# A three-mixer network with expert layers: the overflow branch moved into the block, small loads moved into the mixers, a token tile split earlier

## The chip, the cores and the metric

The kernel runs on one core of a Trainium2 chip. The metric is the time of one execution on the device in microseconds (us), median of several runs. A profile is one further execution, recorded by the hardware profiler.

## The reference, cut to what matters

256 tokens with 1024 features go through three layers. Each layer is a mixer (attention and recurrences of several kinds) followed by a mixture of experts, and the result is normalised once more. The mixers are called even, odd and second here, after the kernel's methods.

```python
for layer in range(2):                       # first_block: even mixer, then odd mixer
    h = _rms(x, norm1_w[layer]) * (1 + scale1) + shift1
    x = x + gate1 * mixer(h)                 # projections, attention, output projection
    h = _rms(x, norm2_w[layer]) * (1 + scale2) + shift2
    x = x + gate2 * _hier_moe(h, ...)        # 32 experts
x = x + second_mixer(rmsnorm(x, attn_norm))  # second_block
x = x + hier_moe(rmsnorm(x, ffn_norm), ...)  # 32 experts again
return rmsnorm(x, final_norm)
```

The experts: a token picks one of 4 groups and in it the best 2 of 8 experts. Each expert e computes `(silu(h @ w1[e]) * (h @ w3[e])) @ w2[e]` with matrices of 1024 x 512, 1024 x 512 and 512 x 1024 floats, 6 MB an expert and 201 MB a layer, all of which is read.

## The kernel before, in words

**Ring and loads.** Weights and large activations share a ring of 18 slots of 1 MB (`ring`, tiles named `slot`). `plan` puts loads on a list in the order of their use, through all layers; `pump` writes the next ones into the program as long as `free > reserve`, all issued by SP (SyncE, L193). `release(n, reserve)` gives n slots back and reserves some of them for activations that will ask for a slot later, `done` gives back the slots of used weights. A load waits on the chip until the last reader of its slot is through.

**Order of landings.** The framework lets eight DMAs be under way. Each DMA, of SP's queue and of ScalarE's, takes the next of eight semaphores in turn, in the order of the program, and waits until the DMA that had it before has landed. Small loads (router weights, constants, the bias) are issued by ScalarE with `nc.scalar.dma_start` and take their turns in the same order.

**A mixer** (`even`, `odd`, `second`) is written by `weave`, which takes steps of several generators (one `stream` of projections, others for heads and normalisations) by estimated costs. `prep` splits weights into a high and a low part (ScalarE, VectorE and GpSimd, L460 to L462) ahead of TensorE's use, up to three chunks ahead. Its last part is `out_last`, the second half of the output projection, token tile 0 and then token tile 1 (tiles of 128 tokens); with token tile 1, `route_turn` and `route_logits` transpose tile 0 and compute its router logits. The transposed tokens hT take one slot.

**An expert block** (`moe`) begins with the reciprocal root of the mean square of all 256 tokens, transposes and router logits of tile 1, and the tokens scaled and split into a high part `hh` and a low part `hl`, one slot each: both high halves on ScalarE (L1775), the low half of tile 0 on GpSimd in two steps (L1778, L1779), that of tile 1 on VectorE (L1782, called `rest`, ahead of the ranks). `route` finds groups, experts and each token's rank within its expert on VectorE, with `warm` multiplications on TensorE between; `finish` computes the weights of the pairs and the largest rank `ti`.

Each expert has room for 64 tokens (`CAP`). `onehot` makes selection matrices for 4 experts, and `gather` multiplies the tokens' halves with them: 32 multiplications on 256 columns give the tokens of 2 pairs of experts, `xg`. If a rank reaches 64, `overflow` computes the remaining tokens of all experts in a loop. It stands between `gather(0)` and the first pair, in a branch on a value which every engine reads:

```python
rv = nc.values_load(ti, min_val=0, max_val=T, ...)
with tc.If(rv >= CAP):
```

The branch isn't taken with these inputs. Behind it every engine adds to semaphores what the body would have added; for the semaphores of DMAs SP does so, each after waiting for its last landing. The body of before has more DMAs than there are semaphores, so all eight are waited for.

Then come 16 pairs of experts. Pair p: `up(p, "g")` (L1840 is its silu), the first half of `combine(p - 1)`, `up(p, "u")` (its end is VectorE's L1844), with odd p `gather` for the next two pairs, `gather_w`, `turn`, the other half of `combine(p - 1)`, `down(p)`. An "up" or "down" has 32 multiplications of 64 columns of weights by 512, and gives its four slots back two at a time, half way and at the end. `parts` splits the result of "down" (VectorE, ScalarE and GpSimd, L1863 to L1865), `combine` multiplies it back to token order and VectorE adds it to x (L1891). At pair 0, behind the first `up`, `start()` is called:

```python
def start1():
    n.gate_coeffs(1, 5)
    n.router(2)
    n.second_setup(pre)
```

`gate_coeffs` broadcasts a row with TensorE and ScalarE, `router` issues 4 small loads, `second_setup` 11 (L1131). `start0` has the bias of the odd mixer (`bias_load`, 1 MB), `gate_coeffs` and `router(1)`. In the third block one load of the final norm's weights stands there.

## Time and profile before

| | |
|---|---|
| median of 3 runs | 2110.97 us (2109.19 to 2112.38) |
| the profiled execution | 2108.36 us |
| its span, first to last instruction | 2106.3 us |
| mean granted TensorE clock, share of full speed | 0.968 |
| TensorE busy | 1901.6 us (90%) |
| VectorE, ScalarE, GpSimd busy | 858.1, 427.5, 327.9 us |
| moved by DMA | 725.35 MB, mean 344 GB/s |

PE is TensorE, PEld its loading of weights, DVE VectorE, ACT ScalarE, POOL GpSimd, SP SyncE; a q behind an engine means its sequencer, which waits, branches and issues DMAs while the engine itself may be busy or idle. Times count from the start of the span. A matrix product in full precision appears as two MATMUL rows.

### The profile page before, as it was taken

To read this page: it belongs to the slowest core of one execution; us is meant where nothing else is said; L and a number is where in the kernel's file an instruction comes from. 1 tells how busy PE (TensorE), PEld (TensorE's weight loads), DVE (VectorE), ACT (ScalarE), POOL (GpSimd) and SP (SyncE) were. 2 spreads that over 40 slices of the span, in tenths; PEclk is the share of its full clock that TensorE was granted. 3 is DMA by queue.
4 is the path that set the end of the run, shared out by engine and by line. 5 is a ranking of instruction groups with operands and counts; after the bars stand their busy time and mean duration, and the time that the engine had idled before them with its cause. 6 is when DMAs were issued, how large, how long until landed. Compare 5 with 4: busy or idle time off the path is not lost. (4 is left out here: it accounts for less than half of the span.)

```text
span 2106.3 us, 24926 instructions
## 1 busy us (share of the span) xinstructions
PE 1901.6 (90%) x9930; PEld 1056.1 (50%) x9930; DVE 858.1 (41%) x1574; ACT 427.5 (20%) x778; POOL 327.9 (16%) x248
## 2 busy tenths in 40 slices
PE   6888799999999899899999999998899899999997
PEld 3656344444444667534444444586788344444443
DVE  3665333333322567533332232467666333232223
ACT  1423101111100343211110011254544111010011
POOL 1331100000000334100000000142444000000000
PEclk8998899999999999999999999998999999999999
DMA  9697799999999856799999999921357799999997
GB/s 323 238 319 297 260 422 421 422 421 421 421 421 406 300 222 244 294 365 421 421 421 421 421 421 421 326 101 41 125 194 300 292 421 421 421 421 422 421 421 285
DMA packets 157547, 725.35 MB, mean 344 GB/s; under 512 B 25305, under 2 KB 43088, under 8 KB 85226
## 3 DMA queue, kind: packets, MB, share of 16 engines
q1 hardware_dynamic: 139216, 716.84, 84.9%
q10 hardware_dynamic: 18201, 6.76, 1.3%
q8 instruction: 85, 1.39, 0.3%
q14 instruction: 45, 0.36, 0.0%
HBM read 722.48 MB, written 1.07 MB: 344 GB/s over the span
## 5 line engine op out<-in xcount | busy, mean ns | idle before, releaser
L257 PE MATMUL ps<-slot,xg 128*64 128x512 f32 x2992 | 710.5, 599 | 20.6 <-DMA slot<-moe_w 9.6
L257 PEld LDWEIGHTS ps<-slot,xg 128*64 128x64 f32 x2992 | 254.4, 138 | 422.0 <-issue 359.8
L257 PE MATMUL ps<-slot,ht 128*64 128x512 f32 (+1 forms) x1552 | 345.0, 574 | 56.4 <-issue 49.2
L257 PE MATMUL ps<-slot 128*128 128x256 f32 (+8 forms) x2230 | 368.4, 327 | 15.1 <-DVE slot L461 9.6
L257 PEld LDWEIGHTS ps<-slot 128*128 128x128 f32 (+3 forms) x2230 | 300.5, 187 | 73.6 <-issue 14.0
L257 PEld LDWEIGHTS ps<-slot,ht 128*64 128x64 f32 x1552 | 128.7, 139 | 228.4 <-issue 213.9
L1891 DVE TENSOR_TENSOR x<-x,ps 128x512 f32<-128x512 f32 x180 | 115.3, 682 | 277.0 <-PE ps L257 277.0
L1865 POOL TENSOR_TENSOR yl<-sg,yh 128x512 fp32r<-128x512 f32 (+1 forms) x68 | 82.5, 1213 | 884.8 <-ACT yh L1864 884.8
L462 POOL TENSOR_TENSOR slot<-slot 128x512 fp32r<-128x512 f32 (+2 forms) x108 | 164.4, 1539 | 273.2 <-ACT slot L460 261.9
L1844 DVE SCALAR_TENSOR_TENSOR hh<-sg,ws,ps 128x512 f32<-128x512 f32 x48 | 53.4, 1113 | 319.4 <-PE ps L257 179.8
L1864 ACT CAST yh<-sg 128x512 fp32r<-128x512 f32 (+1 forms) x68 | 40.3, 593 | 468.9 <-DVE sg L1863 468.9
L461 DVE TENSOR_TENSOR slot<-slot 128x512 fp32r<-128x512 f32 (+2 forms) x108 | 110.2, 1035 | 54.4 <-ACT slot L460 53.9
L1863 DVE TENSOR_TENSOR sg<-ps,ga 128x512 f32<-128x512 f32 (+1 forms) x68 | 44.9, 660 | 175.2 <-PE ps L257 175.2
L460 ACT CAST slot<-slot 128x1024 fp32r<-128x1024 f32 (+2 forms) x108 | 106.6, 1020 | 46.2 <-PE ps L257 27.3
L257 PEld LDWEIGHTS ps<-u,slot 128*128 128x128 f32 x768 | 96.9, 199 | 18.3 <-issue 17.0
L257 PE MATMUL ps<-u,slot 128*128 128x256 f32 x768 | 101.9, 293 | 0.0
L1840 ACT ACTIVATE sg<-ps 128x512 f32<-128x512 f32 x48 | 28.7, 598 | 312.4 <-PE ps L257 312.4
L257 PE MATMUL ps<-yh,pg 128*128 128x512 f32 (+1 forms) x204 | 87.1, 429 | 0.7 <-ACT yh L1864 0.7
L257 PE MATMUL ps<-yl,pg 128*128 128x512 f32 (+1 forms) x204 | 77.5, 382 | 0.9 <-POOL yl L1865 0.8
L1916 POOL TENSOR_TENSOR slot<-x,rows 128x512 f32<-128x512 f32 x2 | 2.5, 1272 | 464.5 <-DVE x L1912 464.5
L398 ACT ACTIVATE xg<-ps,cf 128x256 f32<-128x256 f32 x64 | 36.2, 565 | 156.6 <-PE ps L257 156.6
L1867 ACT CAST yh<-ps 128x512 fp32r<-128x512 f32 (+1 forms) x34 | 19.1, 561 | 227.3 <-PE ps L257 227.2
(334 smaller groups left out, 1586.4 us busy)
## 6 DMA issues: line engine op xcount, KB each, us to landing
slot<-moe_w SPq DMA_DIRECT2D x376, 1024.0 KB, 19.8
slot<-w_gate SPq DMA_DIRECT2D x59, 1024.0 KB, 17.7
slot<-w_up SPq DMA_DIRECT2D x59, 1024.0 KB, 19.8
slot<-w_down SPq DMA_DIRECT2D x50, 1024.0 KB, 18.1
slot<-ada_w SPq DMA_DIRECT2D x48, 1024.0 KB, 7.7
slot<-w_in SPq DMA_DIRECT2D x20, 1024.0 KB, 8.5
slot<-odd_w_in SPq DMA_DIRECT2D x12, 1024.0 KB, 13.1
more<-w_down SPq DMA_DIRECT2D x10, 1024.0 KB, 19.8
```

Source lines behind the costliest of these rows:

```text
L257: self.nc.tensor.matmul(out, lhsT=lhsT, rhs=rhs, start=start, stop=stop)
L398: self.nc.scalar.activation(out, p, AF.Identity, scale=a, bias=nb[:, k:k + 1])
L460: nc.scalar.copy(wh, src)
L461: nc.vector.tensor_sub(wl[:, 0], src[:, 0], wh[:, 0].bitcast(FT))
L462: nc.gpsimd.tensor_sub(wl[:, 1], src[:, 1], wh[:, 1].bitcast(FT))
L1840: nc.scalar.activation(sg, ps, AF.Silu)
L1844: nc.vector.scalar_tensor_tensor(ha.rearrange("s k p -> s p k"), st["sg", p].rearrange("s (p k) -> s p k", k=4), st["ws", p], ps.rearrange ...
L1863: nc.vector.tensor_mul(y, ps, self.ga[:, sl])
L1864: nc.scalar.copy(yh, y)
L1865: nc.gpsimd.tensor_sub(yl, y, yh.bitcast(FT))
L1867: nc.scalar.copy(yh, ps)
L1891: nc.vector.tensor_add(self.x[:, t, sl], self.x[:, t, sl], ps)
```

## The change

The diff does these things.

- **Branch.** `overflow` moves from the front of a block to behind pair 5 (`LATE`). There both halves of `combine(5)` and the gather for pairs 6 and 7 come around it. Its body is rewritten: the transposed tokens go into an `xg` tile, and three loads in a loop replace the earlier ones. hT's slot is given back right behind the router logits.
- **Split.** The slots of `hh` and `hl` are taken in `out_last`. Tile 0's root, high part (ScalarE) and low part (VectorE, two halves) are computed while tile 1 is projected. Tile 1's high part follows on ScalarE, its low part on VectorE in two halves, one before the ranks and one behind the first `onehot`. GpSimd has no part in it.
- **Gather.** `gather(0)` is split into pair 0's columns (before `finish`) and pair 1's (behind `up(0, "u")`). `warm(1)` behind the ranks becomes `warm(2)`.
- **Small loads.** `bias_load` goes into the even mixer, `router(1)` and `second_setup` into the odd one, `router(2)` and the final norm into the second.
- **Reserve.** Three slots are reserved ahead of `out_last` where it was one, and none at the end of a mixer where it was two.

```diff
@@ -26,6 +26,7 @@
 NEG = -1e30
 E = 32
 CAP = 64
+LATE = 5
 RING = 18
 SLOT = 2048
 SCRATCH = 2048
@@ -521,6 +522,8 @@
         setup = self.route_setup()
         next(setup)
         self.hT = self.slot().rearrange("p (k q) -> p k q", k=KC)
+        self.hs = [self.slot(FR).rearrange("p (t k q) -> p t k q", t=NT, k=KC) for i in range(2)]
+        self.hr = self.cp.tile([P, NT], FT, name="xr", bufs=2)
         for t in range(NT):
             for n in range(2):
                 p = self.psum()
@@ -537,9 +540,29 @@
                 self.out_sink(t, n, gate, True)(p)
                 if not t and not n:
                     next(setup)
+                if n and not t:
+                    self.token_rstd(0)
+                    self.token_high(0)
                 if t:
                     (self.route_logits if n else self.route_turn)(0)
+                    self.token_low(0, 4 * n)
                     yield (1.8, 0.0)
+        self.token_rstd(1)
+
+    def token_rstd(self, t):
+        r = self.hr[:, t:t + 1]
+        self.nc.vector.tensor_reduce(r, self.ssq[:, t, :2], axis=AX.X, op=OP.add)
+        self.rstd(r, r, D)
+
+    def token_high(self, t):
+        xv = self.x[:, t].rearrange("q (p k) -> q k p", k=KC)
+        self.nc.scalar.activation(self.hs[0][:, t], xv, AF.Copy, scale=self.hr[:, t:t + 1])
+
+    def token_low(self, t, k):
+        xv = self.x[:, t].rearrange("q (p k) -> q k p", k=KC)
+        hh, hl = self.hs
+        self.nc.vector.scalar_tensor_tensor(hl[:, t, k:k + 4], xv[:, k:k + 4], self.hr[:, t:t + 1],
+                                            hh[:, t, k:k + 4].bitcast(FT), op0=OP.mult, op1=OP.subtract)
 
     def plan_cols(self, key, w, c0, n):
         src = w.rearrange("(p k) n -> p k n", k=KC)[:, :, c0:c0 + n]
@@ -782,7 +805,7 @@
                        p.rearrange("p (h q) -> p h q", h=4))
             yield (0.9, 0.0)
         self.flag("ob", 1.5)
-        self.release(4, reserve=1)
+        self.release(4, reserve=3)
 
     def swa(self, g, bias, sc):
         nc, A = self.nc, self.A
@@ -939,6 +962,7 @@
                 self.gate_coeffs(0, 2)
                 yield (1.8, 5.0)
                 self.router(0)
+                self.bias_load(1, self.bias1)
                 yield from self.mix(self.slab_tm(512, s_vb), 8, self.ev[2])
                 yield from self.mix(self.slab_tm(512, s_rb), 8, self.ev[3])
                 self.release(2)
@@ -958,7 +982,7 @@
             self.weave(self.gla(g, q), self.bias_tile(0, bias, sc), self.swa(g, bias, sc),
                        self.swa_tile(g, 1), self.swa_tile(g, 0),
                        stream())
-        self.release(5, reserve=2)
+        self.release(5)
 
 
     def plan_odd(self):
@@ -1062,6 +1086,8 @@
                 self.outputs(8)
                 yield from self.mix(self.slab_tm(512, s_v(4)), 8, self.od[1])
                 self.gate_coeffs(1, 2)
+                self.router(1)
+                self.second_setup(self.pre)
                 yield (3.8, 0.3)
                 yield from self.mix(self.slab_tm(512, s_qk(3)), 8, self.od[2])
                 yield from self.mix(self.slab_tm(512, s_qk(1)), 8, self.od[3])
@@ -1074,12 +1100,12 @@
                 yield from self.out_half([(self.o[0][:, h], self.o[1][:, h]) for h in range(4)], True)
                 self.prep()
                 yield tuple(("o", h) for h in range(4, 8))
-                self.release(3, reserve=1)
+                self.release(3, reserve=3)
                 yield from self.out_last([(self.o[0][:, h], self.o[1][:, h]) for h in range(4, 8)], True)
 
             self.qkt = {}
             self.weave(*[transposed(s) for s in (2, 0, 3, 1)], *[head(h) for h in range(8)], stream())
-        self.release(6, reserve=2)
+        self.release(6)
 
 
     def plan_second(self):
@@ -1542,6 +1568,7 @@
                 yield from t(h, KC, [[(f, 0, P, s_kraw(1)), (0, P, 152, s_vv(1, 0)), (1, P, 152, s_vv(1, 1))]])
                 self.outputs(4)
                 self.outputs(4)
+                self.router(2)
                 yield from self.slab_fm(4, s_q)
                 yield from self.slab_fm(4, s_f)
                 yield from self.slab_fm(4, s_hq)
@@ -1559,15 +1586,16 @@
                 yield ("hg",)
                 self.mx = [self.slot(FR).rearrange("p (c t) -> p c t", c=8) for i in range(2)]
                 yield from branch(self.o[2:], 1)
-                self.release(3, reserve=1)
+                self.release(3, reserve=3)
                 coeffs()
+                nc.scalar.dma_start(self.rows[1], self.A["final_norm_2"].rearrange("(o n) -> o n", o=1).to_broadcast([P, D]))
                 yield (5.0, 0.0)
                 m = [(self.mx[0][:, k], self.mx[1][:, k]) for k in range(8)]
                 yield from self.out_half(m[:4], False)
                 yield from self.out_last(m[4:], False)
 
             self.weave(self.nsa_prep(g), self.nsa_attn(g, sc), self.hgrn(g, q8), stream())
-        self.release(6, reserve=2)
+        self.release(6)
 
 
     def plan_moe(self, l):
@@ -1669,7 +1697,7 @@
         self.mm(p[:, 0], self.ltri, mk[:, 0], True, True)
         self.mm(p[:, 1], self.ones, mk[:, 0], True, False)
         self.mm(p[:, 1], self.ltri, mk[:, 1], False, True)
-        self.warm(1)
+        self.warm(2)
         rk = g.tile([P, NT, E], FT, name="rk")
         nc.vector.scalar_tensor_tensor(rk, p, 1.0, mk, op0=OP.add, op1=OP.mult)
         nc.vector.tensor_scalar(rk, rk, -1.0, None, op0=OP.add)
@@ -1710,17 +1738,16 @@
         for i in range(n):
             self.mm(p[:, :476], self.ident, self.km, True, True)
 
-    def overflow(self, g, l, hT, h, rk, wt, ti, w1, w3, w2, gate):
+    def overflow(self, g, l, h, rk, wt, ti, w1, w3, w2, gate):
         nc, tc = self.nc, self.tc
-        wd = self.dp.tile([E, P, NT], FT, name="wd", tag="wd")
         rv = nc.values_load(ti, min_val=0, max_val=T, skip_runtime_bounds_check_because="rank < T")
         with tc.If(rv >= CAP):
             wv = g.tile([P, NT, E], FT, name="wv")
             nc.vector.tensor_scalar(wv, rk, float(CAP), None, op0=OP.is_ge)
             nc.vector.tensor_mul(wv, wv, wt)
+            cnt = g.tile([P, 1], FT, name="top")
+            hT = g.tile([P, KC, T], FT, name="xg")
...
+                with tc.For_i(0, 4, 1) as c:
+                    for p, w, tag in zip(pp, (w1, w3), ("yh", "yl")):
+                        nc.scalar.dma_start(wt_, w[bass.ds(e, 1)]...)
...
+                    nc.scalar.dma_start(wt_, w2[bass.ds(e, 1)]...)
...
     def moe(self, l, mods, start, coeffs, slots, fill=None):
         nc, tc = self.nc, self.tc
         _, w1, w3, w2, gate = self.moe_args(l)
         with tc.tile_pool(name="moe", bufs=1, reuse_waits="tile") as g:
-            hT = self.hT
-            hh, hl = (self.slot(FR).rearrange("p (t k q) -> p t k q", t=NT, k=KC) for i in range(2))
-            r = self.x_rstd()
+            hh, hl = self.hs
+            r = self.hr
             self.route_turn(1)
+            self.token_high(1)
             self.route_logits(1)
-            xv = self.x.rearrange("q t (p k) -> q t k p", k=KC)
-            for t in range(NT):
-                nc.scalar.activation(hh[:, t], xv[:, t], AF.Copy, scale=r[:, t:t + 1])
-            h0 = g.tile([P, KC, 2 * P], FT, name="xg").rearrange("p (t k) q -> p t (k q)", t=NT)[:, 0]
-            h0 = h0.rearrange("p (k q) -> p k q", k=KC)
-            nc.gpsimd.tensor_scalar(h0, xv[:, 0], r[:, 0:1], None, op0=OP.mult)
-            nc.gpsimd.tensor_sub(hl[:, 0], h0, hh[:, 0].bitcast(FT))
-
-            def rest():
-                nc.vector.scalar_tensor_tensor(hl[:, 1], xv[:, 1], r[:, 1:2], hh[:, 1].bitcast(FT),
-                                               op0=OP.mult, op1=OP.subtract)
-
-            rk, wt, ti, finish, late = self.route(g, r, mods, rest)
+            self.release()
+            rk, wt, ti, finish, late = self.route(g, r, mods, lambda: self.token_low(1, 0))
             NP = E // 2
             st = {}
             if l == 2:
@@ -1801,18 +1818,19 @@
                 nc.vector.tensor_mul(uw, u, bc(wt, 2 * p, 2))
                 st["uw", p] = uw
 
-            def gather(j):
-                xg = g.tile([P, KC, 2 * P], FT, name="xg")
+            def gather(j, c=slice(0, 2 * P)):
+                if c.start == 0:
+                    st["xg"] = g.tile([P, KC, 2 * P], FT, name="xg")
+                xg = st["xg"]
                 u = st["u", j].rearrange("p t a s -> p t (a s)")
                 for k0 in range(0, KC, 2):
-                    ps = self.psum().rearrange("p (k s) -> p k s", k=2)
+                    ps = self.psum().rearrange("p (k s) -> p k s", k=2)[:, :, :c.stop - c.start]
                     for k in range(2):
                         for t in range(NT):
                             for i, part in enumerate((hh, hl)):
-                                self.mm(ps[:, k], part[:, t, k0 + k], u[:, t], t + i == 0, t + i == 2)
+                                self.mm(ps[:, k], part[:, t, k0 + k], u[:, t, c], t + i == 0, t + i == 2)
                     for k in range(2):
-                        self.affine(xg[:, k0 + k], ps[:, k], k0 + k, "av"[k])
-                st["xg"] = xg
+                        self.affine(xg[:, k0 + k, c], ps[:, k], k0 + k, "av"[k])
 
             def gather_w(p):
                 ps = self.psum((P, T))
@@ -1922,13 +1940,11 @@
                 add(3)
 
             onehot(0)
+            self.token_low(1, 4)
+            gather(0, slice(0, P))
             finish()
-            gather(0)
             if late is not None:
                 late()
-            self.pump()
-            self.overflow(g, l, hT, (hh, hl), rk, wt, ti, w1, w3, w2, gate)
-            self.release()
             weighted(0)
             for p in range(NP):
                 last = p == NP - 1
@@ -1946,26 +1962,30 @@
                     turn(p)
                 else:
                     up(p, "g")
-                    if p:
+                    if p and p - 1 != LATE:
                         combine(p - 1, 0)
-                    else:
+                    elif not p:
                         gather_w(0)
                         start()
-                        if l == 2:
-                            nc.scalar.dma_start(fw, self.A["final_norm_2"].rearrange("(o n) -> o n", o=1)
-                                                .to_broadcast([P, D]))
                     up(p, "u")
-                    if p % 2:
+                    if not p:
+                        gather(0, slice(P, 2 * P))
+                    if p % 2 and p != LATE:
                         gather(p // 2 + 1)
                         if p == NP - 3:
                             self.release(2, reserve=min(2, slots))
                     gather_w(p + 1)
                     turn(p)
-                    if p:
+                    if p and p - 1 != LATE:
                         combine(p - 1, 1)
                 if fill is not None:
                     fill(p)
                 (down_last if last else down)(p)
+                if p == LATE:
+                    combine(p, 0)
+                    combine(p, 1)
+                    self.overflow(g, l, (hh, hl), rk, wt, ti, w1, w3, w2, gate)
+                    gather(p // 2 + 1)
                 if p == NP - 2:
                     coeffs()
             if l == 2:
@@ -2007,30 +2027,17 @@
         n.plan_moe(2)
 
         n.reserve = 6
-        n.even(lambda: n.norm_coeffs(0, 7, 3, 4))
-
         bp = ctx.enter_context(ExitStack())
         n.bias1 = bp.enter_context(tc.tile_pool(name="bias", bufs=1, side="right")).tile([P, 8, T], FT, name="bias1")
-
-        def start0():
-            n.bias_load(1, n.bias1)
-            n.gate_coeffs(0, 5)
-            n.router(1)
-
-        n.moe(0, n.ev[6], start0, lambda: n.norm_coeffs(1, 6, 0, 1), 8,
+        n.even(lambda: n.norm_coeffs(0, 7, 3, 4))
+        n.moe(0, n.ev[6], lambda: n.gate_coeffs(0, 5), lambda: n.norm_coeffs(1, 6, 0, 1), 8,
               lambda p: 4 <= p < 8 and n.bias_flip(n.bias1, n.bias1, p - 4))
+        pb = ctx.enter_context(ExitStack())
+        n.pre = pb.enter_context(tc.tile_pool(name="pre", bufs=1))
         n.odd(lambda: n.norm_coeffs(1, 7, 3, 4))
         bp.close()
         n.rb.close()
-        pb = ctx.enter_context(ExitStack())
-        pre = pb.enter_context(tc.tile_pool(name="pre", bufs=1))
-
-        def start1():
-            n.gate_coeffs(1, 5)
-            n.router(2)
-            n.second_setup(pre)
-
-        n.moe(1, n.od[5], start1, lambda: n.norm_coeffs(1, 8), 14)
+        n.moe(1, n.od[5], lambda: n.gate_coeffs(1, 5), lambda: n.norm_coeffs(1, 8), 14)
         n.fb.close()
         n.second(lambda: n.norm_coeffs(1, 9))
         pb.close()
```

## Rows read from the trace of the kernel before

**Rows 1.** Windows: us, busy us by engine, granted clock, DMA share, GB/s
```profile
224.00:256.00 32.00, 24.64 (x105) 10.16 (x105) 7.42 (x15) 4.75 (x7) 0.00 (x0) 0.86 0.66 235
260.00:670.00 410.00, 381.57 (x1802) 170.91 (x1800) 127.04 (x196) 43.90 (x74) 38.32 (x30) 1.00 1.01 421
876.00:906.00 30.00, 24.02 (x110) 8.80 (x110) 6.94 (x14) 3.87 (x6) 0.00 (x0) 1.00 0.74 251
1630.00:1650.00 20.00, 14.45 (x67) 9.15 (x67) 11.19 (x35) 4.55 (x8) 1.90 (x1) 0.83 0.28 105
```

**Rows 2.** Timeline, VectorE, L1844: start, duration us, shapes [idle before, releaser]
```profile
305.75 1.09 DVE L1844 SCALAR_TENSOR_TENSOR hh<-sg,ws,ps 128x512 f32<-128x512 f32 x1 [6.29 <-issue]
361.31 1.09 DVE L1844 SCALAR_TENSOR_TENSOR hh<-sg,ws,ps 128x512 f32<-128x512 f32 x1 [6.29 <-issue]
...
687.04 1.09 DVE L1844 SCALAR_TENSOR_TENSOR hh<-sg,ws,ps 128x512 f32<-128x512 f32 x1 [2.87 <-PE ps L257]
951.37 1.09 DVE L1844 SCALAR_TENSOR_TENSOR hh<-sg,ws,ps 128x512 f32<-128x512 f32 x1 [6.29 <-issue]
...
1333.33 1.08 DVE L1844 SCALAR_TENSOR_TENSOR hh<-sg,ws,ps 128x512 f32<-128x512 f32 x1 [2.83 <-PE ps L257]
1714.37 1.09 DVE L1844 SCALAR_TENSOR_TENSOR hh<-sg,ws,ps 128x512 f32<-128x512 f32 x1 [6.29 <-issue]
...
2083.07 1.08 DVE L1844 SCALAR_TENSOR_TENSOR hh<-sg,ws,ps 128x512 f32<-128x512 f32 x1 [3.19 <-PE ps L257]
```

**Rows 3.** Waits of SP, 880 to 912 us: releaser, us in total, times, longest
```profile
SPq L193 <- DMA br<-b_grp: 11.1, 1, 11.1
...
SPq L193 <- DMA k_vmask<-k_vmask: 6.9, 1, 6.9
```

**Rows 4.** Waits of SP, 236 to 262 us
```profile
SPq L193 <- DMA bias<-bvec: 6.8, 1, 6.8
```

**Rows 5.** Timeline of the first block's start, 186 to 262 us
```profile
213.55 2.07 DVE L1649 TENSOR_TENSOR oh<-km,i 128x16 f32<-128x16 f32 x1
...
216.68 0.17 DVE L1649 TENSOR_TENSOR oh<-km,i 128x16 f32<-128x16 f32 x1
...
217.25 2.06 DVE L1782 SCALAR_TENSOR_TENSOR slot<-x,xr,slot 128x1024 fp32r<-128x1024 f32 x1
...
218.14 1.04 PE L257 MATMUL ps<-km 128*128 128x476 f32 x2
...
221.09 6.19 PE L257 MATMUL ps<-u,slot 128*128 128x256 f32 x32
...
231.44 9.40 PE L257 MATMUL ps<-slot,xg 128*64 128x512 f32 x32 [4.15 <-issue]
```

**Rows 6.** Timeline of TensorE, 1374 to 1378 us
```profile
1375.16 1.46 PE L257 MATMUL ps<-wx,slot 128*128 128x152 f32 x12
```

**Rows 7.** Timeline of the third block's start
```profile
1645.85 7.09 PE L257 MATMUL ps<-slot,xg 128*64 128x512 f32 x32 [1.82 <-DVEq L1717]
```

**Rows 8.** Source line L1717, the branch: shortest, median, longest ns, first and last start
```profile
L1717 PEldq COMPARE_BRANCH  x3: 3578/3798/3818, 224.9 to 1641.6; - x3
```

**Rows 9.** The page's groups: busy us, mean ns, idle before
```profile
L1865 POOL TENSOR_TENSOR yl<-sg,yh 128x512 fp32r<-128x512 f32 (+1 forms) x68 | 82.5, 1213 | 884.8 <-ACT yh L1864 884.8
```

**Rows 10.** Waits of SP, 380 to 412 us
```profile
SPq L193 <- DMA slot<-moe_w: 27.2, 13, 2.1
```

**Rows 11.** Timeline of ScalarE, 98 to 106 us
```profile
103.51 2.00 ACT L460 CAST slot<-slot 128x1024 fp32r<-128x1024 f32 x2 [2.63 <-DMA wr<-moe_w_expert]
```

**Rows 12.** Timeline of ScalarE, 896 to 902 us: first and last of eleven
```profile
896.04 0.44 ACTq L1131 DMA_DIRECT2D k_rope<-k_rope  x1
...
901.48 0.34 ACTq L1131 DMA_DIRECT2D ll<-hg_lb_logits  x1
```

**Rows 13.** Timeline of the odd mixer, ScalarE and TensorE
```profile
767.26 1.24 ACT L248 COPY pT<-ps 128x384 f32<-128x384 f32 x3 [0.18 <-PE ps L267]
...
769.11 2.17 PE L257 MATMUL ps<-pT,slot 128*128 128x128 f32 x18
```

57 lines of the change are left out of this document (27 added, 30 removed).

## The prediction

> **What bounds the kernel now.** I read the page first and then DMA by stretch, the expert pairs, the queue of the loads, the route, and the mixers' ScalarE. There are three mixers, each followed by an expert block, and the expert blocks are the long plateaus. Inside one the loads move 421 GB/s without a break [rows 1], so a 1 MB load takes 1.049/421 = 2.49 us and a pair of experts (12 loads) 29.9 us. TensorE needs less. Between the pairs 2 and 4 of the first block, at a time when the ring is still full, the step that ends "up" comes 361.31 − 305.75 = 55.6 us apart, 27.8 a pair [rows 2]. From pair 2 to pair 15 that would be 13 × 27.8 = 361 us, and it takes 381.3, 382.0 and 368.7 us in the three blocks [rows 2]. So TensorE waits about 20, 21 and 8 us for weights in the later pairs: the end of a block is set by its last load, and what counts is how early the loads become continuous. Time that TensorE loses early is free up to those 20, 21 and 8 us.
>
> Before each plateau the loads limp: 235 GB/s over 32 us at the first block, 251 over 30 at the second, 105 over 20 at the third [rows 1]. At 421 this is (421−235)/421 × 32 = 14.1 us of idle DMA, 12.1 and 15.0. Two causes. All slots are full and the first is given back only half way through the first "up", and in the first two blocks SP then stands still: every load waits for the landing of the DMA eight before it, of whatever queue, and the small loads that ScalarE issues there take places in this order. SP waited 11.1 and 6.9 us for them at the second block [rows 3], 6.8 us for bias1 at the first [rows 4].
>
> **The start of a block.** In the first block, GpSimd's subtraction holds up a VectorE step to 2.07 us where the same instruction takes 0.17 later; without GpSimd −1.9. The low half of token tile 1 costs 2.06 us ahead of the ranks; half of it stays there, −1.0. Ranks are then 2.9 us earlier, but a second warm-up multiplication (1.04 us) now stands between them and the gather, so this starts some 2.6 us earlier. It took 6.19 us, 193 ns a multiplication, with the granted clock at its lower level for part of it (0.86 over the stretch, rows 1) [rows 1, 5]. The first half has the same 32 multiplications on 128 columns; the nearest row, 152 columns, has twelve in 1.46 us, 122 ns [rows 6], and with the overlap at its end I take 110, 3.5 us: −2.7. Then TensorE idled 4.15 us at the branch [rows 5]; in its place come the last affine step, the maximum of the ranks and one small multiplication, some 1.5 us: −2.65. Against this, tile 0's high part (I take the present 2.1 us on ScalarE) comes ahead of ScalarE's copies in the last projections, and a VectorE half of 1.0 us ahead of the last reduction: +1.1. The first "up" begins 6.9 us earlier, and runs in 7.09 as in the third block instead of 9.40 [rows 5, 7]. In the third block clock and branch cost less (there TensorE's pause is 1.82 us, rows 7), and the same terms give −4.2. Bounds: 0 (if the ScalarE work costs 4) to 9 us.
>
> What does it give? First block: 14.1 us idle, plus the 2.5 of bias1, which leaves this stretch, minus 5.0 for two loads that the larger reserve (3 slots, not 1) pushes into it: 11.6. The late gather half adds 3.5 us of TensorE but covers 1.5 us of waiting for VectorE; it delays the "down" slots by 2, still in time for the DMA. Second block: 12.1 + 2.2 for the 0.9 MB of small loads − 5.0 + about 1 us of idle DMA before that stretch: 10 (bounds 5 to 13). Third: no small load held SP, so the loads gain the 4.2 us and 1.2 of the final norm's half MB, 5.4, if TensorE follows.
>
> The Trainium skill (TensorE: Matmul & The Clock Gate, "Back-to-back issue gap") says that streaming time goes with the number of columns, with a sustained spacing of 81 ns at 128. By it a half gather takes 2.6 us, an estimate, and the third block gains 0.9 us more; the trace's 152-column row speaks against it, and my sum goes by the row.
>
> **The late branch.** TensorE's branch instruction takes 3.6 to 3.8 us [rows 8], now partly covered by queued multiplications. At pair 5 it stands behind "combine", which itself waits for the parts of "down": VectorE, then ScalarE, then GpSimd's 1.2 us [rows 9], some 3 us uncovered; then about 3.5 us of branch, and the gather behind it no longer covers VectorE's step (1.0). I sum 7.5 us (5.8 in the third block, where the parts are shorter); bounds 4 and 12, with 2.3 us of slower clock as in rows 5. Behind the branch wait the gather and "up" of pair 6. Cover: TensorE's waiting later in the block. First block: 20 + 6.9 − 2 − 7.5 = 17, more than the 11.6 gained, and likewise in the second, so all of it stays. Third: 8 + 4.2 − 2 − 5.8 = 4.4, less than 5.4, so 4.4. SP branches too, and waits there for three places of the order of eight, the oldest; in this stretch it waits for landings of its own loads anyway (27.2 of 32 us) [rows 10], so five stay in flight, 12 us of data, and DMA doesn't pause.
>
> **The small loads in the mixers.** In the odd mixer ScalarE issues 4 router loads (2.6 us of waiting ScalarE in the even mixer, which issues its own already) [rows 11] and 11 for the last mixer (896.04 to 901.82, 5.8 us) [rows 12] right behind the gate copies. That is 8.4 us in which ScalarE starts nothing. Queued behind: a weight cast of 1.05 us and the copies pT, at 767.26 now, and TensorE's multiplications at 769.11 need pT [rows 13]. ScalarE is ready some 1 to 1.5 us ahead there, so TensorE stands 7 us, and some 1 us goes in slower clock: 8 lost (bounds 1 and 12). In the last mixer 2.6 us, beside work that is queued for TensorE: 1.5 (0 to 3.5). In the even mixer one bias load: 0.4.
>
> **Sum.** 11.6 + 10 + 4.4 − 8 − 1.5 − 0.4 = 16.1 us less than the profiled execution's 2108.36 (span 2106.3): 2092.3. The median of the runs, 2110.97, lies 2.6 above this execution, so I say 2095.
>
> **Rivals.** *Small loads hidden (14%).* If the odd mixer's queued work covers ScalarE, 8 becomes 1: 2088. For: casts of weights run up to three chunks ahead of their use. Against: pT is used 2 us after its copy begins [rows 13], and TensorE works in order.
>
> *A dear branch (12%).* With 3 us more at each late branch and 12 in the odd mixer, 2095 + 3 + 4 = 2102. For: the 4.15 us pause was followed by the slower 9.40 us "up" [rows 5]; against: after the 1.82 us of the third block it was 7.09 [rows 7].
>
> *The branch drains the queue (8%).* If SP waits at the join for all loads in flight, as now, DMA idles per block for about 4.3 us (I take the 6.8 us for which SP stood at the first block, rows 4, less one load's 2.49). The first two lose 8.6: 2104. The edit to three loads would then not do what it says. The Trainium skill (Runtime: NRT & Kernel Launch, "Instruction fetch mechanics") has a rule here: a taken branch to a page not yet fetched stalls the engine. The trace shows it on TensorE in all three branches; for SP it would add to this case alone.
>
> *Slower (16%): the small loads hold SP in the mixers as they now do at the blocks.* If loads of a mixer's weights come behind them, SP stands 18.0 us in the odd mixer [rows 3] and 6.8 in each of the others [rows 4], 31.6 in place of 9.9, and TensorE runs dry: 26.0 − 31.6 is a loss of 5.6, 2117. It decides as soon as the mixers together lose over 26 us. For: fifteen DMAs go twice round the order of eight. Against: at the blocks SP waited because ScalarE issued late and DMA was saturated; in the mixers it is neither.
>
> **Chances.** Forecast 50% (its own range 2086 to 2104). About 0.2%, 4.2 us, is what a measurement can tell. Of the cases, forecast, hidden, dear and drained make it faster but for their tails: 75% faster, 10% the same, 15% slower. The range runs from 2081, where the hidden case meets a cheap start, to 2114, which takes in half of the slower case.
>
> **What would show it.** Loads at 421 GB/s from the first "up" of each block; no SP wait for small loads in the blocks; first "up" 7 (third: 4) us after its mixer earlier than now; pairs 5 to 6 some 7 us longer, and later pairs less starved; a 7 us hole in TensorE where the odd mixer's gate copies end. It is wrong if the plateau begins no earlier, if DMA falters at pair 5, or if TensorE waits for weights in a mixer.

## The result and the profile after

The changed kernel takes 2087.59 us (median of four runs, 2084.17 to 2091.31) against 2110.08 of the kernel before: ratio 0.9897, interval 0.9872 to 0.9922, 22.5 us less. The profiled executions span 2085.8 and 2106.3 us.

First the windows of the kernel after, at the places of [rows 1] (us, busy us by engine, granted clock, DMA share, GB/s):

```profile
224.00:256.00 32.00, 27.74 (x148) 14.12 (x148) 11.85 (x35) 7.01 (x14) 0.00 (x0) 0.95 0.93 374
260.00:665.00 405.00, 378.12 (x1816) 167.10 (x1812) 127.24 (x196) 43.89 (x74) 38.46 (x30) 0.99 1.01 420
865.00:895.00 30.00, 27.30 (x145) 13.91 (x143) 10.69 (x32) 7.01 (x14) 0.00 (x0) 0.94 1.00 402
1622.00:1642.00 20.00, 19.03 (x108) 8.88 (x106) 6.20 (x24) 4.93 (x9) 0.00 (x0) 1.00 0.77 308
```

The limping 235, 251 and 105 GB/s ahead of the three plateaus have become 374, 402 and 308 (329 over 1611 to 1631 us, which lies to the third block's first "up" as the window of before does); the plateau is 420 as before. At the starts of the first two blocks SP waits for slots and for no small load. Next the VectorE step that ends "up" (L1862 now), of pairs 0 and 15 of each block, which answers to [rows 2]:

```profile
249.37 1.12 DVE L1862 SCALAR_TENSOR_TENSOR hh<-sg,ws,ps 128x512 f32<-128x512 f32 x1 [9.20 <-PE ps L258]
678.52 1.09 DVE L1862 SCALAR_TENSOR_TENSOR hh<-sg,ws,ps 128x512 f32<-128x512 f32 x1 [2.88 <-PE ps L258]
890.67 1.12 DVE L1862 SCALAR_TENSOR_TENSOR hh<-sg,ws,ps 128x512 f32<-128x512 f32 x1 [9.20 <-PE ps L258]
1321.96 1.08 DVE L1862 SCALAR_TENSOR_TENSOR hh<-sg,ws,ps 128x512 f32<-128x512 f32 x1 [2.87 <-PE ps L258]
1641.25 1.13 DVE L1862 SCALAR_TENSOR_TENSOR hh<-sg,ws,ps 128x512 f32<-128x512 f32 x1 [6.03 <-PE ps L258]
2064.04 1.08 DVE L1862 SCALAR_TENSOR_TENSOR hh<-sg,ws,ps 128x512 f32<-128x512 f32 x1 [2.85 <-PE ps L258]
```

These steps cut the span into seven stages. The table has them in us for every kernel that was run, from one profile each, with the ratio of its time to that of the kernel before. Stages of the same code differ by up to 4.5 us between executions (the first one, with the same even mixer, is 249.5 in e9 and 245.1 in e11), mostly where the granted clock fell to its lower level at other moments; a stage difference below that carries nothing by itself.

| kernel | to block 1 | block 1 | odd mixer | block 2 | last mixer | block 3 | rest | ratio (interval) |
|---|---|---|---|---|---|---|---|---|
| before | 251.8 | 435.2 | 210.4 | 435.9 | 327.1 | 422.6 | 23.2 | 1 |
| after | 249.4 | 429.2 | 212.2 | 431.3 | 319.3 | 422.8 | 21.8 | 0.9897 (0.9872, 0.9922) |
| e1 | 247.1 | 431.9 | 214.0 | 430.8 | 318.7 | 422.5 | 21.8 | 0.9908 (0.9886, 0.9930) |
| e2 | 246.0 | 429.1 | 203.6 | 443.7 | 322.3 | 422.5 | 23.4 | 0.9925 (0.9907, 0.9942) |
| e3 | 251.8 | 430.0 | 216.0 | 431.1 | 327.1 | 421.6 | 22.0 | 0.9976 (0.9965, 0.9986) |
| e4 | 249.7 | 428.9 | 212.5 | 429.5 | 319.2 | 420.8 | 23.5 | 0.9881 (0.9864, 0.9899) |
| e5 | 245.4 | 441.4 | 204.5 | 450.4 | 322.5 | 422.4 | 23.4 | 0.9983 (0.9966, 1.0000) |
| e6 | 249.7 | 430.7 | 217.6 | 429.0 | 324.2 | 422.6 | 23.4 | 0.9950 (0.9931, 0.9968) |
| e7 | 245.3 | 435.3 | 213.5 | 435.3 | 321.7 | 430.1 | 21.8 | 0.9996 (0.9982, 1.0010) |
| e8 | 242.2 | 435.6 | 204.0 | 447.5 | 322.2 | 421.1 | 23.5 | 0.9975 (0.9958, 0.9992) |
| e9 | 249.5 | 429.0 | 206.1 | 430.7 | 322.6 | 422.9 | 22.2 | 0.9889 (0.9869, 0.9910) |
| e10 (of before) | 252.1 | 434.8 | 210.5 | 438.0 | 326.3 | 423.2 | 21.5 | 1.0019 (1.0005, 1.0033) |
| e11 | 245.1 | 431.2 | 214.6 | 430.7 | 319.2 | 422.6 | 22.1 | 0.9926 (0.9905, 0.9946) |
| e12 | 245.7 | 427.8 | 204.9 | 427.4 | 318.2 | 420.8 | 22.2 | 0.9843 (0.9821, 0.9865) |

How a block is read: where TensorE waits for no weights, it takes 24.8 us from pair 0 to 1, then 29.1 and 26.5 in turn, and 27.7 for the last, 415.2 in all. In the first two blocks the last pair also has 16 multiplications for the next mixer's norm, which take 4.0 us in every kernel, and the half "up" behind them depends on the clock. Here are these rows of block 1 before, of block 1 after, and the half "up" of block 2 after:

```profile
663.89 3.99 PE L257 MATMUL ps<-km,rows 128*128 128x16 f32 x16
667.81 6.24 PE L257 MATMUL ps<-slot,xg 128*64 128x512 f32 x16
```
```profile
657.94 3.98 PE L258 MATMUL ps<-km,rows 128*128 128x16 f32 x16
661.84 3.65 PE L258 MATMUL ps<-slot,xg 128*64 128x512 f32 x16
...
1302.40 6.56 PE L258 MATMUL ps<-slot,xg 128*64 128x512 f32 x16
```

The 6.24 and 6.56 were mostly at the lower clock (granted 0.58 and 0.55), the 3.65 at the full one. Before, the blocks took 435.2, 435.9 and 422.6, which is 20, 21 and 7 us over 415.2. Of this 4.0 in each of the first two is the norm's work and 2.6 and 1.4 the clock behind it, so that 13.4, 15.3 and 7.4 us were waiting for weights. After, the late half gather adds 3.3 to the first interval (28.1) and the late branch 6.6, 4.0 and 4.3 to those from pair 5 to 7 (62.1, 59.5 and 59.8 against 55.5). With the norm's 4.0 (and, in block 2, 2.9 of lower clock) nothing is left over in the first block, 2 us in the second and nothing in the third. So some 13 us of waiting went in each of the first two blocks and 10 and 7 of TensorE's own work came in; in the third 7 went and 7.5 came. The pages say the same of the whole span: the idle time ahead of the multiplications of "up" fell from 20.6 to 0.2 us, and the time in which they were under way from 710.5 to 687.5.

```profile
L257 PE MATMUL ps<-slot,xg 128*64 128x512 f32 x2992 | 710.5, 599 | 20.6 <-DMA slot<-moe_w 9.6
L258 PE MATMUL ps<-slot,xg 128*64 128x512 f32 x2992 | 687.5, 599 | 0.2 <-DMA slot<-moe_w 0.2
```

The start of the first block, TensorE and the branch, answer to [rows 5, 8]:

```profile
224.20 3.93 PE L258 MATMUL ps<-u,slot 128*128 128x128 f32 x32
229.35 0.38 PE L258 MATMUL ps<-km,top 128*1 128x128 f32 x2 [1.22 <-DVE ge L1716]
229.66 8.78 PE L258 MATMUL ps<-slot,xg 128*64 128x512 f32 x32
...
249.16 3.79 PE L258 MATMUL ps<-u,slot 128*128 128x128 f32 x32
```
```profile
L1744 PEldq COMPARE_BRANCH  x3: 318/344/352, 403.4 to 1793.9; - x3
```

In place of the 4.15 us pause ahead of "up" there is a single multiplication behind a pause of 1.22. The gather took 3.93 us at full clock (granted 1.00 over 224.2 to 228.1 us), where the 6.19 of [rows 5] were at the lower one (0.61 over 221.0 to 227.3). The first "up" took 8.78 us, granted 0.81, and 7.09 only in the third block. The branch instruction takes 0.34 us, not 3.8. The odd mixer, ScalarE and TensorE, answers to [rows 13]:

```profile
755.21 0.57 ACTq L1620 DMA_DIRECT2D wr<-moe_w_group  x1
...
763.00 0.48 ACTq L1157 DMA_DIRECT2D ll<-hg_lb_logits  x1
763.52 1.05 ACT L461 CAST slot<-slot 128x1024 fp32r<-128x1024 f32 x1 [7.73 <-DMA k_causal<-k_causal]
764.47 1.23 ACT L249 COPY pT<-ps 128x384 f32<-128x384 f32 x3
...
764.99 4.17 PE L258 MATMUL ps<-pT,slot 128*128 128x128 f32 x18 [6.06 <-ACT pT L249]
```

ScalarE issues for 8.3 us, TensorE stands 6.06, and its 18 multiplications then take 4.17 instead of 2.17. SP is held too, much longer, in 740 to 862 us:

```profile
SPq L194 <- DMA k_csel<-k_csel: 30.4, 1, 30.4
```

That cost nothing that shows: in the kernel before SP issued no load from 741.3 to 763.4 us either, for want of a slot, and from 700 to 870 us TensorE waited for no landing.

### The profile page after: what moved, and what is told of

Its sections match the earlier page's. It is cut to its first block, busy times and chain, and to the rows that moved or that the text cites. A ratio compares the mean times of both kernels' runs of the same rounds, so it can differ in the third digit from the quotient of the medians.

```text
span 2085.8 us, 25140 instructions
## 1 busy us (share of the span) xinstructions
PE 1889.9 (91%) x10032; PEld 1042.9 (50%) x10032; DVE 862.6 (41%) x1601; ACT 431.7 (21%) x790; POOL 310.3 (15%) x245
## 5 line engine op out<-in xcount | busy, mean ns | idle before, releaser
L258 PE MATMUL ps<-slot,xg 128*64 128x512 f32 x2992 | 687.5, 599 | 0.2 <-DMA slot<-moe_w 0.2
L258 PEld LDWEIGHTS ps<-slot,xg 128*64 128x64 f32 x2992 | 232.8, 138 | 396.5 <-issue 379.1
L463 POOL TENSOR_TENSOR slot<-slot 128x512 fp32r<-128x512 f32 (+2 forms) x108 | 164.2, 1537 | 278.4 <-ACT slot L461 226.7
L1862 DVE SCALAR_TENSOR_TENSOR hh<-sg,ws,ps 128x512 f32<-128x512 f32 x48 | 53.4, 1113 | 318.6 <-PE ps L258 204.3
L258 PEld LDWEIGHTS ps<-u,slot 128*128 128x128 f32 x864 | 104.3, 192 | 23.4 <-issue 17.0
L258 PE MATMUL ps<-u,slot 128*128 128x256 f32 (+1 forms) x864 | 109.6, 285 | 3.5 <-DVEq L1744 3.5
L399 ACT ACTIVATE xg<-ps,cf 128x256 f32<-128x256 f32 (+1 forms) x72 | 38.9, 540 | 169.2 <-PE ps L258 169.2
```

Source lines behind the costliest of these rows:

```text
L258: self.nc.tensor.matmul(out, lhsT=lhsT, rhs=rhs, start=start, stop=stop)
L399: self.nc.scalar.activation(out, p, AF.Identity, scale=a, bias=nb[:, k:k + 1])
L463: nc.gpsimd.tensor_sub(wl[:, 1], src[:, 1], wh[:, 1].bitcast(FT))
L1862: nc.vector.scalar_tensor_tensor(ha.rearrange("s k p -> s p k"), st["sg", p].rearrange("s (p k) -> s p k", k=4), st["ws", p], ps.rearrange ...
```

## Experiments

All are edits of the kernel after, but e10; the code is shortened. Ratios are to the kernel before; the kernel after has 0.9897.

**e1: the load of bias1 back at the first block.**

```
-                self.bias_load(1, self.bias1)        # even mixer
+        def start0(): n.bias_load(1, n.bias1); n.gate_coeffs(0, 5)
```


> The kernel after, with the load of bias1 (1 MB) issued at the start of the first expert block again, as before; all else as after. Theory A: in the kernel after this megabyte runs ahead of a weight load that ScalarE's cast waits for; that is the 1.8 us step at 121 us, the slower clock behind it 2.5 us more. Then the first 'up' begins 4 to 5 us earlier than after (near 225 us), while the block takes back the 2.5 us of transfer and some of SP's 6.8 us of waiting: 2083 to 2089 us. Theory B, the prediction's: the load costs the even mixer 0.4 us; the step at 121 us is something else and stays, the first 'up' stays within 1 us of 229.7, and the block loses 2.5 to 6.8 us: 2090 to 2094 us.

0.9908: no difference to after. TensorE at the disputed place of the even mixer, in the kernel before, after and in e1:

```profile
121.14 1.77 PE L257 MATMUL ps<-slot 64*128 64x256 f32 x11 [0.75 <-DVE slot L250]
```
```profile
122.87 2.40 PE L258 MATMUL ps<-slot 64*128 64x256 f32 x11 [2.57 <-DVE slot L251]
```
```profile
122.09 1.77 PE L258 MATMUL ps<-slot 64*128 64x256 f32 x11 [1.20 <-DVE slot L251]
```
Without the megabyte the pause is 1.20 us and the multiplications run at full speed, so it was the megabyte; block 1 then begins 2.3 us earlier (not 4 to 5) and takes 2.7 longer, both within what executions differ by. Theory A's place is right, and in the time the two places of the megabyte can't be told apart.

**e2: the other small loads back at the blocks.**

```
-                self.router(1); self.second_setup(self.pre)   # odd mixer
-                self.router(2)                                # last mixer
+        start0: n.router(1)      start1: n.router(2); n.second_setup(n.pre)
```


> The kernel after, with the router loads of the odd and the last mixer and the 11 loads for the last mixer issued at the starts of the first two expert blocks again, as before; bias1 stays in the even mixer. Theory A, the prediction's: in the odd mixer these loads hold ScalarE and cost 7.5 us there, more than their 0.9 MB (2.2 us) and SP's waits cost at the start of the second block, so the odd mixer is 6 to 8 us shorter and the second block 4 to 8 us longer: 2083 to 2090 us, no clear loss. Theory B: taking the 18 us of SP waits out of the blocks is what the change gains by, and they all come back as idle DMA: 6 to 12 us slower than after, 2094 to 2100 us.

0.9925, some 6 us slower than after: between the two. The odd stretch is 8.6 us shorter, as A said; block 2 is 12.4 longer, not 4 to 8. SP's longest wait in 855 to 905 us and the window after the first "up", in e2 (in the kernel after 875 to 900, which lies to the first "up" as this window does, moved 382 GB/s):

```profile
SPq L194 <- DMA wr<-w_grp: 21.8, 1, 21.8
```
```profile
865.00:890.00 25.00, 19.30 (x98) 9.10 (x96) 5.16 (x12) 3.27 (x7) 0.00 (x0) 0.90 0.62 202
```
(421 − 202)/421 × 25 = 13 us of idle DMA against 2: bunched at a block, the small loads cost more than ScalarE's time in the mixer.

**e3: the branch ahead of pair 0 again.**

```
-                if p == LATE: combine(p, 0); combine(p, 1); self.overflow(...); gather(p // 2 + 1)
+            self.overflow(...)      # behind the first half gather and late()
```


> The kernel after, with the branch on an overflow ahead of pair 0 of each block again (behind the first half of the gather) instead of behind pair 5. Theory A, the prediction's: the first 'up' of each block begins 3 to 5 us later, pairs 5 to 7 are 7.4, 3.9 and 4.2 us shorter; in the first two blocks the loads set the end, so the later start is lost and the shorter pairs gain nothing; in the third the two about cancel: 2091 to 2098 us. Theory B: TensorE's time decides in every block, what is lost at the start comes back at pair 5: 2085 to 2090 us.

0.9976, 14 to 17 us slower than after. SP's waits near the second block's start, TensorE's branch, TensorE at the first block, and the windows, all of e3:

```profile
SPq L1743 <- DVE pgr L1722: 9.2, 1, 9.2
```
```profile
L1744 PEldq COMPARE_BRANCH  x3: 334/415/444, 228.8 to 1637.9; - x3
```
```profile
231.07 5.39 PE L258 MATMUL ps<-slot,xg 128*64 128x512 f32 x12 [3.35 <-DVEq L1744]
```
```profile
224.00:256.00 32.00, 26.02 (x129) 12.56 (x128) 9.02 (x30) 6.56 (x13) 0.00 (x0) 0.89 0.82 317
868.00:898.00 30.00, 24.01 (x112) 10.63 (x110) 8.88 (x30) 5.18 (x10) 0.00 (x0) 0.89 0.90 349
```
An early branch holds two engines: SP stands 9.2 us for the value (16.0 in the third block), loads fall to 317 and 349 GB/s, and TensorE stands 3.35 us. Block 1 has no late-branch work and still takes 430.0: beside the last pair's 4.0 and 1.5 of lower clock, 6 us are waiting. Theory A, and more than it expected. The edit also gives hT's slot back only behind the branch, as before; what that one slot is worth is not separated.

**e4: the whole first gather ahead of pair 0.**

```
-            gather(0, slice(0, P))   ...   if not p: gather(0, slice(P, 2 * P))
+            gather(0)
```


> The kernel after, with the whole first gather (256 columns) ahead of pair 0 instead of one half there and one behind its 'up'. Theory A, the prediction's: the first 'up' begins 2 to 3 us later in each block, pair 0 is 2.5 to 3.5 us shorter for TensorE; the first two blocks, bound by loads, lose 2 to 3 us each, the third is even: 2090 to 2095 us. Theory B: TensorE's time decides, and the halves cost 32 more matmuls per block: 2083 to 2087 us.

0.9881, 2082.48 us: theory B's side, half a microsecond below its range; A's 2 to 3 us per block do not exist. Its interval overlaps that of the kernel after, so the gain itself isn't clear. The gather of 256 columns in e4, and the late one after pair 5 of the first and second block in the kernel after:

```profile
225.76 4.15 PE L258 MATMUL ps<-u,slot 128*128 128x256 f32 x32
```
```profile
405.77 6.18 PE L258 MATMUL ps<-u,slot 128*128 128x256 f32 x32 [1.33 <-DVEq L1744]
...
1046.57 4.00 PE L258 MATMUL ps<-u,slot 128*128 128x256 f32 x32 [1.09 <-DVEq L1744]
```
Half the columns take 3.79 to 3.93 us, all of them 4.00 to 4.15; the 6.19 of [rows 5] and the 6.18 here were at the lower clock (granted 0.89 over 396 to 428 us). The halves buy nothing and cost 3.3 us of TensorE. Yet of these 3.3 us the first two blocks give back only 0.3 and 1.8: in block 1 of e4 TensorE waits for weights again, as here, ahead of the last 14 multiplications of pair 13's "up".

```profile
611.51 3.65 PE L258 MATMUL ps<-slot,xg 128*64 128x512 f32 x14 [0.72 <-DMA slot<-moe_w]
```

**e5 and e8: one small load per expert pair**, with the first gather in halves and whole.

```
+        fill0(p): p == 1: bias_load;  8 <= p < 12: one router-1 load
+        fill1(p): 1 <= p < 13: one second_setup or router-2 load;  p == 13: the rest
```


> The kernel after, with the small loads neither in the mixers nor at the starts of the blocks but one per expert pair, behind the pair's turn: bias1 in pair 1 and router 1 in pairs 8 to 11 of the first block; the 11 loads for the last mixer and the router's first in pairs 1 to 12 of the second block, the other three in pair 13. Theory A: what the small loads cost is ScalarE's time in the odd mixer (7.5 us), the megabyte ahead of a weight load in the even mixer (3 to 4 us), and, bunched in a block, two rounds of the order of eight with hardly a byte in flight. One among seven megabytes costs only its bytes (2 MB, 4.7 us over two blocks): the odd mixer is 6 to 8 us shorter, no SP wait over 3 us for a small load; 2077 to 2084 us. Theory B: the order of eight charges every small load a whole place of 2.5 us, 16 of them 40 us of a load's turn: the two blocks are 5 to 20 us longer each, 2088 to 2105 us.

> The kernel with the loads spread over the pairs (as the run e5_spread) and the whole first gather ahead of pair 0 (as e4_whole_gather). Theory A: the two gains add, 3 us of the gather and those of e5_spread: 2074 to 2081 us. Theory B: both gains are TensorE's time in blocks whose ends the loads set, so the second adds nothing: within 1.5 us of e5_spread.

0.9983 and 0.9975: theory B for e5, one microsecond past its range. The odd stretch is 8 us shorter, but blocks 1 and 2 are 12 and 19 us longer than after. Waits of SP in the second block of e5 (two of eight for small loads, 93 us together), and its windows:

```profile
SPq L195 <- DMA wr<-w_grp: 18.6, 1, 18.6
SPq L195 <- DMA k_csel<-k_csel: 15.2, 1, 15.2
```
```profile
260.00:670.00 410.00, 379.71 (x1788) 168.85 (x1786) 124.72 (x193) 42.64 (x72) 36.87 (x29) 0.99 1.00 412
900.00:1320.00 420.00, 382.27 (x1792) 168.96 (x1788) 125.37 (x191) 42.71 (x72) 37.38 (x30) 0.98 0.98 402
```
SP runs ahead of ScalarE, so each small load, issued late by ScalarE, stops SP when its turn in the order of eight comes round. e8 lies 20 us over theory A's range, since e5 gained nothing, and gains 2 to 4 us on e5 against theory B's 1.5, which doesn't decide it.

**e6: token tile 0 scaled in the block again.**

```
-                if n and not t: self.token_rstd(0); self.token_high(0)     # out_last
-                    self.token_low(0, 4 * n)
+            self.token_high(0) ... rest: token_low(0, 0), token_low(0, 4), token_low(1, 0)
```


> The kernel after, with the scaling and the low part of token tile 0 taken out of the last projections and put at the start of the block, beside tile 1's (ScalarE 2 us, VectorE two halves of 1.03 us more there). Theory A, the prediction's: the mixers end 1 to 1.5 us earlier, the first 'up' begins 2 to 3 us later after them; net 1 to 2 us lost in each block: 2089 to 2094 us. Theory B: at the start of a block VectorE and ScalarE have the time (both wait for logits and ranks), nothing lost, and the mixers' 1 to 1.5 us is won: 2083 to 2086 us.

0.9950, 11 us slower than after, twice what theory A said. VectorE and TensorE at the second block's start in e6:

```profile
866.03 3.23 DVE L561 SCALAR_TENSOR_TENSOR slot<-x,xr,slot 128x512 fp32r<-128x512 f32 x3
...
870.50 6.23 PE L258 MATMUL ps<-u,slot 128*128 128x128 f32 x32 [1.73 <-DVE u L1809]
```
Three low parts stand ahead of the ranks, TensorE pauses 1.73 us, and the gather behind it takes 6.23 us, mostly at the lower clock (granted 0.57), instead of 3.93.

**e7 and e10: ten idle multiplications behind pair 5**, in the kernel after and in the kernel before.

```
+                    self.warm(10)
```


> The kernel after, with ten idle multiplications more (476 columns, each some 0.8 us) on TensorE in front of the late branch of each block, about 8 us of TensorE's time in the middle of a block. Theory A, the prediction's: a block whose loads set its end takes such time for nothing up to what TensorE still waits in the last pairs (in the kernel after some 4 us in the first block, 7 in the second, none in the third): 2 to 5, 0 to 2 and 7 to 9 us, together 2098 to 2104 us. Theory B: no cover is left anywhere, TensorE sets every block's end: 24 us, 2108 to 2113 us.

> The kernel before, with ten idle multiplications on TensorE behind pair 5 of each block; in the kernel after the same ten took 7.1 us each time and made the whole 21 us slower. Theory A, the prediction's reading of the kernel before: loads set the ends of its blocks, and TensorE's 20, 21 and 7 us of waiting cover the pad: 0 to 1 us in each of the first two blocks, 0 to 3 in the third, together 0 to 5 us over the kernel before. Theory B: TensorE sets the ends here too: 14 to 22 us slower.

In the kernel before, the ten took TensorE 8.3 us in each block (first line), 25 us in all, and cost 0.19%, 4 us: theory A. In the kernel after, they made the way from pair 5 to 6 longer by 7.2 us in the last two blocks, and by 4.5 in the first, where the gather behind them no longer fell to the lower clock; the time grew by some 21 us: theory B, at the lower end of its range. Its blocks grow 6.1, 4.0 and 7.3 us. The 4.1 and 7.0 us by which the last pairs of blocks 1 and 2 exceed 27.7 in the kernel after are 5.8 in both blocks of e7: the norm's 4.0 again, and a half "up" of 5.35 us, partly at the lower clock (granted 0.68). Only the second block's 2 us of waiting took up any of the added work.

```profile
401.89 8.25 PE L257 MATMUL ps<-km 128*128 128x476 f32 x20
```
```profile
662.18 5.35 PE L258 MATMUL ps<-slot,xg 128*64 128x512 f32 x16
```

**e9 and e11: the odd mixer's 15 small loads issued by SP, or by GpSimd.**

```
-                self.router(1)                     -            nc.scalar.dma_start(self.S[nm], src)
+                self.router(1, nc.sync)            +            nc.sync.dma_start(self.S[nm], src)     # e11: nc.gpsimd
```


> The kernel after, with the 15 small loads of the odd mixer issued by SP instead of ScalarE, at the same place of the program. In the traces so far ScalarE issues them in 8.3 us, and the stretch from the last 'up' of the first block to the first of the second is 212 to 214 us with them and 203 to 205 us in the runs that have them elsewhere. Theory A: it is ScalarE's time that the odd mixer pays, and nothing else: the stretch falls to 203 to 206 us, and since the second block then runs at TensorE's pace but for some 9 us at its end, at least half of it is kept: 4 to 9 us faster than after, 2077 to 2083 us. Theory B: the 8.3 us of issuing only change place; SP's weight loads come later by as much and TensorE waits for weights: the stretch stays over 210 us, 2085 to 2090 us.

> As e9_sp_queue, but the 15 loads are issued by GpSimd, which is busy 15% of the span and has the low parts of the weights to compute in this mixer. Theory A: as there, the stretch falls to 203 to 206 us, 2077 to 2083 us. Theory B: GpSimd's low parts of the weights wait behind the issuing, and TensorE for them: the stretch stays over 210 us, 2085 to 2092 us.

e9: 0.9889, the odd stretch 206.1, theory A's stage. Its last mixer was 3.3 us longer than after's, at a mean granted clock of 0.94 against 0.96, so that its whole gain isn't clear of after. e11: 0.9926, theory B. TensorE in the odd mixer, first e9, then e11:

```profile
758.76 2.17 PE L258 MATMUL ps<-pT,slot 128*128 128x128 f32 x18
```
```profile
772.84 1.22 PE L258 MATMUL ps<-slot 128*128 128x512 f32 x2 [6.18 <-POOL slot L463]
```
On SP the pause is gone, and SP waits for no small load in this mixer; on GpSimd the pause has moved to the low parts of the weights (L463), which wait behind the issuing.

**e12: e9 and e4 together.**

> The kernel after, with the odd mixer's 15 small loads on SP (as e9_sp_queue) and the whole first gather ahead of pair 0 (as e4_whole_gather). Each of the two took single microseconds off the span, which the comparison of the runs leaves inside its interval. Theory A: the two are in different stages (odd mixer 6 us; TensorE's 3.3 us in pair 0, of which the third block keeps 2), and add: the odd stretch 206 us, the third block 421 us, 2076 to 2081 us. Theory B: what is won ahead of the first two blocks is waited for again in their last pairs, where loads still decide, and only the third block's 2 us are kept: 2083 to 2087 us, no faster than the kernel after beyond the interval.

0.9843 (2071.54 us), the fastest of all, clear of the kernel after and some 11 us below it. The odd stretch (204.9) and block 3 (420.8) are as A said; 5 us more came ahead of block 1 and in the last mixer, which the edits hardly touch; over 1335 to 1640 us the granted clock was 0.97, against 0.96 after. Both gains are there in one run; why the whole is more than their sum is open.

## Why the prediction was right, and where it wasn't

**Right: what bounded the kernel before.** Loads set the ends of its blocks: e10 gives TensorE 25 us more to do for 4. The prediction saw that the third block would be TensorE's after the change (422.8 against 422.6, nothing gained inside).

**Too large: the cover.** The 20 and 21 us of TensorE's waiting came from a pace that leaves out the norm's work in the last pair; 13.4 and 15.3 were waiting. With these the prediction's own working leaves 13.4 + 6.9 − 2 − 7.5 = 10.8 us of cover in the first block, less than the 11.6 gained, and 12.7 in the second, so that 0 and 2.7 us of waiting should be left instead of some 5 and 8; the trace has 0 and 2. So what it said of the third block holds for all three: more work on TensorE now costs its full time (e7). Less work gains little in the first two blocks (e4): loads and TensorE end there at nearly the same time.

**Right in size: the odd mixer.** 8 us said; ScalarE issues for 8.3, the stretch is 6 to 9 us shorter wherever the loads are issued by SP or at another place (e2, e5, e9). The rival that hid them falls. The slower rival was half right: a small load held SP for 30.4 us, more than the 18.0 that rival counted with, but TensorE did not run dry, since SP had no slot to fill there before either. The odd stretch is 212.2.

**Right in size for a wrong reason: the late branch.** 7.5, 7.5 and 5.8 said, 6.6, 4.0 and 4.3 measured, the last two near the lower bound of 4. But 3.5 of it was to be the branch instruction, which takes 0.34. In the first block the wait for the parts (0.73 and 0.86 us for GpSimd's), 1.3 behind the branch, 2.2 of slower clock in the gather and 0.9 at VectorE's step make 6.0 of the 6.6. The drained queue did not happen: SP waited 6.4 us at the branch in 380 to 420 us while DMA moved 420 GB/s.

**Near in size, not in its terms: the start.** 6.9, 6.9 and 4.2 said; from the end of the last projections to the first "up" 7.7, 5.7 and 6.1 us went (25.7, 23.7 and 23.1 before; 18.0, 18.0 and 17.0 after). In the first block these are the last projections, before and after:

```profile
202.74 2.99 PE L257 MATMUL ps<-slot 128*128 128x512 f32 x12
```
```profile
208.65 2.99 PE L258 MATMUL ps<-slot 128*128 128x512 f32 x12
```

The 6.9 takes 2.6 us from ranks that are 2.9 earlier and a multiplication of 1.04 between, without saying why not 1.9. The half gather (−2.7) was worth nothing (e4): the gather did get 2.3 us shorter, but by the full clock. The split of the token tile was worth more than its VectorE microsecond, since without it TensorE pauses and its clock falls (e6, 11 us in all). And a cause of the limping loads is missing: beside full slots and small loads, SP stood for the branch's value, 7.4, 7.1 and 15.7 us ahead of the three blocks of before. The prediction priced TensorE's idle 4.15 at the branch, not this; e3, which brings it back, loses 14 to 17 us.

**Wrong: the bias load, 0.4 us.** It is a megabyte in front of a weight load: TensorE's pause there grew from 0.75 to 2.57 us and its clock fell (granted 0.57 over 122.8 to 130.8 us); the twelve multiplications that ended at 126 us before ended at 131, 4.9 us later. In the whole time this can't be told from what the same megabyte costs in the block (e1).

**Sum.** At the end of each block the change was 8.5, 11.4 and 19.0 us ahead (11.2, 13.2 and 16.1 said), and 20.5 at the end. The first two fall short by 2.7 and 1.8 us, no more than the same code differs by (with the same even mixer e2 and e7 have the first of these steps at 246.0 and 245.3 us, the kernel after at 249.4). The last is over by the last mixer's stretch, 7.8 us shorter where 2.7 were said: 6.1 of it is the start. The clock may account for the rest (mean granted 0.96 against 0.94 over 1335 to 1640 us); which of it the change causes isn't settled. e3, e6 and e2 undo 15, 11 and 6 us, more than the 22.5 of the whole: the parts are not independent. The larger reserve and the second warm-up multiplication were undone by no run, so that the 5.0 us charged for the reserve in each of the first two blocks are not shown.

The Trainium skill (TensorE: Matmul & The Clock Gate, "Back-to-back issue gap") would have half the columns in 2.6 us, an estimate from its 81 ns a multiplication; the trace has 3.79 to 3.93 for 128 columns and 4.00 for 256, and the measurement decides.

## What to carry to other kernels

Work out how much an engine waits from the places where the trace shows it waiting, not from a pace taken elsewhere in the stage: work that comes once, at the end, looks like waiting and is no cover. An added dummy on the engine, in both kernels, shows in one run each whether the bound has changed sides. A branch on a value held not only the engine that computes but also the one that issues the loads; put it where loads are in flight. Small loads belong on the engine that has nothing due in that stage, at a place that it reaches early, and not one by one on a second engine among loads that share an order.

## What the runs showed of the hardware

TensorE's branch over the overflow code fell from 3.6 to 3.8 us to 0.32 to 0.44 us, in both places (after and e3), so it isn't the place. With the body of before it took 3.3 to 3.4 us in e10 too; the rewritten body, with its inner loops, is what the quick ones share. The Trainium skill (Runtime: NRT & Kernel Launch, "Instruction fetch mechanics") has a taken branch to a page not yet fetched stall the engine, which would fit a shorter jump; the trace has only the time of the branch, and no run here shows what was fetched.

A multiplication of 128 columns took nearly as long as one of 256 (3.79 to 3.93 against 4.00 us for 32). And the same 15 loads take 8.3 us to issue on ScalarE; 11 of them take 5.5 there and 5.4 on SP (740.98 to 746.39 in e9), while on GpSimd the 15 stretch over 19 us (752.28 to 771.50 in e11), with waits for earlier ones in between.
